# Attention scores of 64-wide heads in split precision: from three matmuls on 64 partitions to two on 128

## The chip, the cores and the metric

The kernel runs on one core of one Trainium2 chip. The metric is the device time of one execution in microseconds (us), the median of several runs. The kernel before takes 2592.72 us (three runs: 2592.72, 2592.72 and 2596.87).

## What is computed

The reference is a stack of four layers over one sequence of 512 tokens of 1024 channels: two layers of a first kind and two of a second, all in fp32. Two parts matter here, one in each kind of layer.

```
# first kind: differential attention, 4 heads, each with two maps m of width 64, v of width 128
scores = einsum('bqhmd,bkhmd->bhmqk', qb, kh)          # causal, block of 128 queries
p = softmax(where(mask, scores, -inf))
w = p[:, :, 0] - lam * p[:, :, 1]
out = einsum('bhqk,bkhd->bqhd', w, vf)

# second kind: sliding-window attention, 8 heads of width 64 over 2 key heads, window 128
sc = (q . k) - slope * distance, masked to the window   # 128 queries see at most 256 keys
p = softmax(concat(sc, sink)); o = p @ v
```

Around them stand large projections (1024 to 8208 columns and to 4256 columns), a state-space scan, a second attention with heads of width 96, and a feed-forward layer.

## The kernel before

All of the program is recorded first, call by call, in an object `Order` (lines 118 to 382). It then issues the calls in the order of a list schedule: each engine takes, among the calls whose operands are there by the schedule's own costs, the one with the highest priority, which is the place in the program with a bonus for weight loads and evictions. Line 379 issues every instruction, so every row of the profile names L379, and groups are told apart by the names of their tiles. The costs of the schedule (line 157, `cost`) do not run on the chip, but they decide in what order each engine's fixed stream stands. For a split-precision matmul of n columns the cost is max(n / 2.4 + 2.5, 109) ns (line 166).

Matmuls that need nearly fp32 accuracy are done in split precision: an fp32 operand is split into a high part (type fp32r, written by ScalarE) and a low part (fp32 minus the high part, by VectorE), and `mm3` (line 501) issues three matmuls, high by high, high by low and low by high, into one PSUM tile. Projections (`tm`, `fm`) contract 128 partitions at a time and write the PSUM tiles `pm`; everything else writes tiles `px`, of which there are four. Weights come from memory as `wr` on SyncE's queue and are split into `wh` and `wl`.

Scores have contraction width 64. In the first kind of layer, `qk_norm` (line 846) transposes q and k on TensorE, two maps of a head on one tile of 128 partitions (map 0 on partitions 0 to 63, map 1 on 64 to 127), and splits each into `qkh` and `qkl`; it also keeps the first 128 tokens in plain fp32 (`qkf`). `da_attn` (line 863) then loops over the four query blocks i, inside over the four heads and the two maps. For i = 0 one plain fp32 matmul on 64 partitions makes the 128x128 scores (TensorE runs it as two passes, so the trace shows two records); for i = 1 to 3 the three matmuls of `mm3` work on 64 partitions with 256, 384 and 512 columns. So a layer has 8 fp32 matmuls (16 records) and 8 x 3 x 3 = 72 split ones: 88 records of 64 partitions. Each score tile goes to VectorE (bias, minimum) and ScalarE (exponential) as `p`, the weighted difference is transposed (`px<-ident,p`), copied to `pt` and multiplied with `vv`.

In the second kind, `swa_norm` (line 1206) and `swa_attn` (line 1228) do the same for the sliding window with tiles `sqth`, `sqtl`, `skth`, `sktl`, `sqf` and `skf`: 8 heads, i = 0 in fp32 with 128 columns, i = 1 to 3 with three matmuls of 256 columns: again 16 + 72 = 88 records a layer. What follows in the program is, in the first kind, the projection for z and the gates, and in the second kind, two gate projections recorded just ahead of it and the attention with heads of width 96 (`mqh`, `mql`, contraction over 96 partitions). The schedule puts matmuls of these projections between the attention's.

GpSimd issues only parameter loads (`pn`, `pa`, `pb`, `pc`, `mw`, `ab`), 25 in all, through its own queue.

Of the kernel before, what the change touches and what calls it, by code (L numbers as in the profile page):

```python
# [19 lines left out]
P = 128  # L20
# [97 lines left out]
class Order:  # L118
    """Records the engine calls of a program, then issues them in the order of a list schedule:
    each engine takes, among the calls whose operands are there, the one that the program has first."""  # L120
# [36 lines left out]
    def cost(self, key, name, out, ins, kw):  # L157
# [4 lines left out]
        if key == "pe":  # L162
            if name == "transpose":
                return 107.0
            if ins[0].dtype == F32R:
                return max(n / 2.4 + 2.5, 109.0)
            return 2 * max(n / 1.2 + 2.5, 109.0)
# [217 lines left out]
class Kern:  # L385
# [173 lines left out]
    def norm(self, x, gain, spill=True):  # L559
        """The rows scaled by the gain only, split in two; their 1/rms by token, as a column and over partitions;  # L560
        and a function that makes the split of the wholly scaled rows."""
# [283 lines left out]

    def qk_norm(self, raw, ms):
        nc = self.nc
        dst = []
# [7 lines left out]
        first = self.slot("qkf")  # L856
        for h in range(4):
            ps = self.transpose_to(raw, h * P)
            nc.scalar.copy(out=first[:, h * P:(h + 1) * P], in_=ps[:, 0:P])
            dst.append(self.split(ps, "qk"))  # L860
        return dst, first

    def da_attn(self, q, qt, kt, v):
        nc = self.nc
        (qt, qf), (kt, kf) = qt, kt
        yc = []
        for i in range(NT):
            n = (i + 1) * P
            o = self.slot("yc")
            for h in range(4):  # L870
# [3 lines left out]
                for m in range(2):  # L874
                    ps = self.pmix()
                    s = slice(m * 64, m * 64 + 64)
                    if i == 0:
                        hs = slice(h * P, (h + 1) * P)
                        nc.tensor.matmul(ps[:, :n], qf[s, hs], kf[s, hs], start=True, stop=True)
                    else:  # L880
                        c = slice(i * P, (i + 1) * P)
                        self.mm3(ps[:, :n], qt[h][0][s, c], qt[h][1][s, c], kt[h][0][s, 0:n], kt[h][1][s, 0:n], True, True)
# [10 lines left out]
                for b in range(i + 1):  # L893
                    nc.tensor.matmul(po[:, 0:P], pt[:, b * P:(b + 1) * P], v[b][:, h * P:(h + 1) * P],
                                     start=(b == 0), stop=(b == i))
                nc.scalar.activation(out=o[:, h * P:(h + 1) * P], in_=po[:, 0:P], func=AF.Copy, scale=rr[:, 0:1])
# [10 lines left out]
            yc.append(o)  # L907
        return yc

    def layer1(self, l, x):  # L910
# [61 lines left out]
        qt = self.qk_norm(qr, msq)  # L972
        kt = self.qk_norm(kr, msk)
        yc = self.da_attn(q, qt, kt, vv)
# [231 lines left out]
    def swa_norm(self, q, sraw, sk, msq, msk):  # L1206
# [11 lines left out]
        qf, kf = self.slot("sqf"), self.slot("skf", [P, P])  # L1218
        ps = self.transpose_to(sk, 0)
        nc.scalar.copy(out=kf, in_=ps[:, 0:P])  # L1220
        kt = self.split(ps, "skt")
        for j in range(4):
            ps = self.transpose_to(sraw, j * P)
            nc.scalar.copy(out=qf[:, j * P:(j + 1) * P], in_=ps[:, 0:P])
            qt.append(self.split(ps, "sqt"))
        return (qt, qf), (kt, kf)

    def swa_attn(self, q, qt, kt, sk, gs, rx):
        nc = self.nc
        (qt, qf), (kt, kf) = qt, kt  # L1230
        y = []
        for i in range(NT):
# [6 lines left out]
            for hp in range(4):  # L1239
                s = hp // 2  # L1240
                sl = slice(s * 64, s * 64 + 64)
                ps = self.pmix()
                for e in range(2):
                    j = (hp * 2 + e) % 4
                    if i == 0:
                        nc.tensor.matmul(ps[:, e * 256:e * 256 + n], qf[sl, j * P:(j + 1) * P], kf[sl, :], start=True, stop=True)
                    else:
                        c = slice(i * P, (i + 1) * P)
# [232 lines left out]
```

## Time and profile before

| | |
|---|---|
| median of the runs | 2592.72 us |
| span of the profiled execution | 2608.1 us (no time of its own is listed beside the span) |
| TensorE matmuls | 2597.5 us, 12708 records |
| weight loads (PEld) | 2191.3 us |
| VectorE | 1587.9 us (61%) |
| ScalarE | 1093.2 us (42%) |
| GpSimd | 13.7 us (1%) |
| DMA | mean 96 GB/s |

The profile is one execution, so its times stand against its own span of 2608.1 us and not against the median. Matmuls are pipelined: the duration that a row shows (0.39 us for 512 columns) reaches into the next one, so TensorE is "busy" all the time, and what a matmul costs is read from the distance between the starts of neighbours in the timeline. In the view by windows, the x after an engine is how many records fall into the stretch, and PEclk is the granted TensorE clock as a share of 2.4 GHz.

### The profile page before, as it was taken

The page shows a single profiled execution, that of the slowest core. Times are in us where ns is not written, and L with a number is a line of the kernel's source. Part 1 is how long each engine was busy: PE and PEld are TensorE (multiplying, and loading weights), DVE is VectorE, ACT ScalarE, POOL GpSimd, SP SyncE. Part 2 cuts the span into 40 slices and gives each one's busy share as a digit, 9 for nine tenths or more (in the row PEclk, how much of TensorE's full clock was granted, in tenths as well). Part 3 has the DMA queues.
Part 4 walks back from the last instruction along what each step waited for, and adds up shares of the span by engine and source line. Part 5 has one row for each costly group of instructions (what it writes and reads, how often), then busy time and mean ns, then how long its engine had stood idle before and what let it go on. Part 6 is the DMA issues. An engine that isn't in the chain of part 4 may idle for free.

```text
span 2608.1 us, 33396 instructions
## 1 busy us (share of the span) xinstructions
PE 2597.5 (100%) x12708; PEld 2191.3 (84%) x12708; DVE 1587.9 (61%) x3165; ACT 1093.2 (42%) x2006; POOL 13.7 (1%) x29
## 2 busy tenths in 40 slices
PE   9999999999999999999999999999999999999999
PEld 7898788888888888987888888888898988988987
DVE  7689843368555356798533585553496655875562
ACT  5443723235443244436332344442345723534632
POOL 0000000000000000000000000000000000000000
PEclk9999999999999999999999999999999999997999
DMA  7333143343333343331333433334432124330132
GB/s 224 79 69 73 40 123 91 95 156 103 97 97 115 130 107 83 80 63 49 89 89 97 132 126 97 96 96 146 135 84 65 28 73 157 100 97 17 33 100 94
DMA packets 154815, 249.79 MB, mean 96 GB/s; under 512 B 10320, under 2 KB 70112, under 8 KB 154400
## 3 DMA queue, kind: packets, MB, share of 16 engines
q1 hardware_dynamic: 152864, 241.03, 33.1%
q0 software_dynamic: 1792, 6.63, 0.8%
q8 instruction: 100, 1.64, 0.3%
q14 instruction: 59, 0.48, 0.1%
HBM read 232.94 MB, written 14.68 MB: 95 GB/s over the span
## 4 chain that ended last, share of the span: by engine, by line
PE 99%; DMA 0%; SPq 0%; ACT 0%; issue 0%; DVE 0%
PE pm L379 76%; PE px L379 23%; DMA wr<-in_w_in_dram 0%; DMA xr<-xd 0%; SPq L379 0%; ACT wh L379 0%; DVE xt L379 0%; ACT pt L379 0%
## 5 line engine op out<-in xcount | busy, mean ns | idle before, releaser
L379 DVE TENSOR_TENSOR wl<-wr,wh 128x1024 fp32r<-128x1024 f32 (+3 forms) x413 | 489.8, 1186 | 836.8 <-ACT wh L379 817.3
L379 ACT CAST wh<-wr 128x1024 fp32r<-128x1024 f32 (+3 forms) x413 | 422.6, 1024 | 1009.7 <-PE pm L379 818.5
L379 PE MATMUL pm<-hh,wl 128*128 128x512 f32 x896 | 349.3, 390 | 0.0
L379 PE MATMUL pm<-hl,wh 128*128 128x512 f32 x896 | 349.1, 390 | 0.0
L379 PE MATMUL pm<-hh,wh 128*128 128x512 f32 x896 | 348.7, 390 | 0.0
L379 PEld LDWEIGHTS pm<-hh,wl 128*128 128x128 f32 x896 | 168.3, 188 | 34.8
L379 PEld LDWEIGHTS pm<-hh,wh 128*128 128x128 f32 x896 | 168.3, 188 | 34.7 <-issue 0.3
L379 PEld LDWEIGHTS pm<-hl,wh 128*128 128x128 f32 x896 | 168.3, 188 | 34.5
L379 PE MATMUL pm<-gh,wh 128*128 128x512 f32 x384 | 153.8, 401 | 0.0
L379 PE MATMUL pm<-gl,wh 128*128 128x512 f32 x384 | 153.6, 400 | 0.0
L379 PE MATMUL pm<-gh,wl 128*128 128x512 f32 x384 | 153.3, 400 | 0.0
L379 PE MATMUL pm<-wh,gh 128*128 128x512 f32 (+2 forms) x384 | 141.4, 371 | 1.4 <-ACT wh L379 1.2
L379 PE MATMUL pm<-wl,hh 128*128 128x384 f32 (+2 forms) x384 | 142.6, 371 | 0.0
L379 PE MATMUL pm<-wl,gh 128*128 128x512 f32 (+2 forms) x384 | 141.5, 369 | 0.0
L379 PE MATMUL pm<-wh,hl 128*128 128x384 f32 (+2 forms) x384 | 141.3, 368 | 0.0
L379 PE MATMUL pm<-wh,hh 128*128 128x384 f32 (+2 forms) x384 | 141.1, 368 | 0.0
L379 PE MATMUL pm<-wh,gl 128*128 128x512 f32 (+2 forms) x384 | 140.9, 368 | 0.0
L379 PE MATMUL pm<-acth,wh 128*128 128x512 f32 x352 | 137.0, 389 | 0.0
L379 PE MATMUL pm<-actl,wh 128*128 128x512 f32 x352 | 137.0, 389 | 0.0
L379 PE MATMUL pm<-acth,wl 128*128 128x512 f32 x352 | 136.7, 389 | 0.0
L379 PE MATMUL px<-hh,wl 128*128 128x512 f32 x320 | 124.6, 389 | 0.0
L379 PE MATMUL px<-hl,wh 128*128 128x512 f32 x320 | 124.6, 389 | 0.0
(440 smaller groups left out, 5156.3 us busy)
## 6 DMA issues: line engine op xcount, KB each, us to landing
wr<-in_w_in_dram SPq DMA_DIRECT2D x151, 512.0 KB, 3.8
wr<-in_ffn_w_up_dram SPq DMA_DIRECT2D x176, 256.0 KB, 3.1
wr<-in_ffn_w_down_dram SPq DMA_DIRECT2D x44, 512.0 KB, 3.5
wr<-in_w_out_dram SPq DMA_DIRECT2D x40, 512.0 KB, 3.6
wr<-in_w_in_dram SPq DMA_DIRECT2D x40, 384.0 KB, 3.6
xr<-xd SPq DMA_DIRECT2D x48, 256.0 KB, 5.0
xd<-xr SPq DMA_DIRECT2D x40, 256.0 KB, 3.7
wr<-in_w_branch_b_dram SPq DMA_DIRECT2D x16, 512.0 KB, 3.5
```

The lines of the kernel that those rows point to most:

```text
L379: ins = f(*args, **kw).ins
```

## The change

Scores are now made by `scores`: two matmuls that contract 128 partitions. The stationary operand is a query tile `qk` (or `sqt`) for one map or head alone, with its high part on one half of the partitions and its low part on the other (`stack_q`). The moving operands are two key tiles, `qkh` and `qkl` (`skth`, `sktl`), each with the same 64 rows on both halves (`stack_k`). The two products give all four terms, high by high, low by high, high by low and low by low. The query's low part is written by VectorE straight to the other half of the partitions; the key's second half is a copy by DMA, 64 rows of 2 KB, issued by GpSimd. The plain fp32 tiles for i = 0 are gone; all four blocks take this way. `da_attn` now loops over heads outside and over query blocks inside, and transposes and stacks a head's q and k at the start of its turn; the norm of the outputs comes after all heads. Lastly the schedule's cost of a split-precision matmul is max(n / 2.4 + 13.4, 109) ns.

```diff
@@ -163,7 +163,7 @@
             if name == "transpose":
                 return 107.0
             if ins[0].dtype == F32R:
-                return max(n / 2.4 + 2.5, 109.0)
+                return max(n / 2.4 + 13.4, 109.0)
             return 2 * max(n / 1.2 + 2.5, 109.0)
         aps = sum(1 for k in ("scale", "bias", "scalar", "scalar1", "scalar2") if isinstance(kw.get(k), bass.AP))
         if key == "act":
...
@@ -843,9 +843,35 @@
             ys.append(yh)
         return ys
 
+    def stack_k(self, ps, rows, name):
+
+        nc = self.nc
+        other = slice(64 - rows.start, 128 - rows.start)
+        h, l = self.slot(name + "h", dt=F32R), self.slot(name + "l", dt=F32R)
+        nc.scalar.copy(out=h[rows, :], in_=ps[rows, :])
+        nc.vector.tensor_sub(out=l[rows, :], in0=ps[rows, :], in1=h[rows, :].bitcast(F32))
+        nc.gpsimd.dma_start(out=h[other, :], in_=h[rows, :])
+        nc.gpsimd.dma_start(out=l[other, :], in_=l[rows, :])
+        return h, l
+
+    def stack_q(self, ps, rows, name):
+
+        nc = self.nc
+        other = slice(64 - rows.start, 128 - rows.start)
+        t = self.slot(name, dt=F32R)
+        nc.scalar.copy(out=t[rows, :], in_=ps[rows, :])
+        nc.vector.tensor_sub(out=t[other, :], in0=ps[rows, :], in1=t[rows, :].bitcast(F32))
+        return t
+
+    HALVES = (slice(0, 64), slice(64, 128))
+
+    def scores(self, ps, q, k):
+        nc = self.nc
+        nc.tensor.matmul(ps, q, k[0], start=True, stop=False)
+        nc.tensor.matmul(ps, q, k[1], start=False, stop=True)
+
     def qk_norm(self, raw, ms):
         nc = self.nc
-        dst = []
         nc.vector.tensor_scalar_add(out=ms, in0=ms, scalar1=EPS)
         r = self.rsqrt(ms, NT * 8)
         for t in range(NT):
...
@@ -853,33 +879,21 @@
             nc.vector.tensor_tensor(out=r3, in0=r3,
                                     in1=r[:, t * 8:(t + 1) * 8].unsqueeze(2).to_broadcast([P, 8, HD]), op=ALU.mult)
             self.rope(r3[:, :, 0:16], 8, 8, self.rope1, t)
-        first = self.slot("qkf")
+    def da_attn(self, q, qr, kr, v):
+        nc = self.nc
+        yc = [self.slot("yc") for _ in range(NT)]
         for h in range(4):
-            ps = self.transpose_to(raw, h * P)
-            nc.scalar.copy(out=first[:, h * P:(h + 1) * P], in_=ps[:, 0:P])
-            dst.append(self.split(ps, "qk"))
-        return dst, first
-
-    def da_attn(self, q, qt, kt, v):
-        nc = self.nc
-        (qt, qf), (kt, kf) = qt, kt
-        yc = []
-        for i in range(NT):
-            n = (i + 1) * P
-            o = self.slot("yc")
-            for h in range(4):
+            hs = slice(h * P, (h + 1) * P)
+            kt, qt = [[f(ps, rows, "qk") for rows in self.HALVES]
+                      for f, ps in ((self.stack_k, self.transpose_to(kr, h * P)), (self.stack_q, self.transpose_to(qr, h * P)))]
+            for i in range(NT):
+                n = (i + 1) * P
                 mn = self.small("mn", 2)
                 ss = self.small("ss", 2)
                 pr = []
                 for m in range(2):
                     ps = self.pmix()
-                    s = slice(m * 64, m * 64 + 64)
-                    if i == 0:
-                        hs = slice(h * P, (h + 1) * P)
-                        nc.tensor.matmul(ps[:, :n], qf[s, hs], kf[s, hs], start=True, stop=True)
-                    else:
-                        c = slice(i * P, (i + 1) * P)
-                        self.mm3(ps[:, :n], qt[h][0][s, c], qt[h][1][s, c], kt[h][0][s, 0:n], kt[h][1][s, 0:n], True, True)
+                    self.scores(ps[:, :n], qt[m][:, i * P:(i + 1) * P], [k[:, 0:n] for k in kt[m]])
                     pr.append(self.softmax_block(ps[:, :n], self.mask[:, T - n:], HD ** -0.5, 3.0e38,
                                                  mn[:, m:m + 1], ss[:, m:m + 1], n))
                 rr = self.small("rr", 2)
...
@@ -891,9 +905,10 @@
                 pt = self.transpose_p(pr[0], i + 1, "s")
                 po = self.pmix()
                 for b in range(i + 1):
-                    nc.tensor.matmul(po[:, 0:P], pt[:, b * P:(b + 1) * P], v[b][:, h * P:(h + 1) * P],
+                    nc.tensor.matmul(po[:, 0:P], pt[:, b * P:(b + 1) * P], v[b][:, hs],
                                      start=(b == 0), stop=(b == i))
-                nc.scalar.activation(out=o[:, h * P:(h + 1) * P], in_=po[:, 0:P], func=AF.Copy, scale=rr[:, 0:1])
+                nc.scalar.activation(out=yc[i][:, hs], in_=po[:, 0:P], func=AF.Copy, scale=rr[:, 0:1])
+        for o in yc:
             ms = self.small("oms", 4)
             sq = self.slot("osq")
             nc.scalar.activation(out=sq, in_=o, func=AF.Square, scale=128 ** -0.5)
...
@@ -969,9 +983,9 @@
         self.tm(w, C_DT + 400, 384, h, ev1)
         self.tm(w, C_DT + 784, 384, h, ev2)
         self.tm(w, C_DT + 1168, 384, h, ev3)
-        qt = self.qk_norm(qr, msq)
-        kt = self.qk_norm(kr, msk)
-        yc = self.da_attn(q, qt, kt, vv)
+        self.qk_norm(qr, msq)
+        self.qk_norm(kr, msk)
+        yc = self.da_attn(q, qr, kr, vv)
         msz = self.small("msz", 2 * NT)
 
         def ev_z(hf):
...
@@ -1215,19 +1229,15 @@
             nc.vector.tensor_tensor(out=s3, in0=s3, in1=rq[:, t * 8:(t + 1) * 8].rearrange("p (s j) -> p s j", s=2).unsqueeze(3).to_broadcast([P, 2, 4, HD]), op=ALU.mult)
             k3 = sk[t][:, 0:128].rearrange("p (s d) -> p s d", d=HD)
             nc.vector.tensor_tensor(out=k3, in0=k3, in1=rk[:, t * 2:(t + 1) * 2].unsqueeze(2).to_broadcast([P, 2, HD]), op=ALU.mult)
-        qf, kf = self.slot("sqf"), self.slot("skf", [P, P])
         ps = self.transpose_to(sk, 0)
-        nc.scalar.copy(out=kf, in_=ps[:, 0:P])
-        kt = self.split(ps, "skt")
+        kt = [self.stack_k(ps, rows, "skt") for rows in self.HALVES]
         for j in range(4):
             ps = self.transpose_to(sraw, j * P)
-            nc.scalar.copy(out=qf[:, j * P:(j + 1) * P], in_=ps[:, 0:P])
-            qt.append(self.split(ps, "sqt"))
-        return (qt, qf), (kt, kf)
+            qt.append([self.stack_q(ps, rows, "sqt") for rows in self.HALVES])
+        return qt, kt
 
     def swa_attn(self, q, qt, kt, sk, gs, rx):
         nc = self.nc
-        (qt, qf), (kt, kf) = qt, kt
         y = []
         for i in range(NT):
             ss = self.small("sss", 8)
...
@@ -1238,16 +1248,11 @@
             k0 = max(i - 1, 0) * P
             for hp in range(4):
                 s = hp // 2
-                sl = slice(s * 64, s * 64 + 64)
                 ps = self.pmix()
                 for e in range(2):
                     j = (hp * 2 + e) % 4
-                    if i == 0:
-                        nc.tensor.matmul(ps[:, e * 256:e * 256 + n], qf[sl, j * P:(j + 1) * P], kf[sl, :], start=True, stop=True)
-                    else:
-                        c = slice(i * P, (i + 1) * P)
-                        self.mm3(ps[:, e * 256:e * 256 + n], qt[j][0][sl, c], qt[j][1][sl, c],
-                                 kt[0][sl, k0:k0 + n], kt[1][sl, k0:k0 + n], True, True)
+                    self.scores(ps[:, e * 256:e * 256 + n], qt[j][s][:, i * P:(i + 1) * P],
+                                [k[:, k0:k0 + n] for k in kt[s]])
                 pp = []
                 for e in range(2):
                     h = hp * 2 + e
```

The schedule makes a new order from this. Three places show it. In the first layer's attention, TensorE's stream of before holds the block i = 1 of two heads so (`px_647` and `px_649` are the two maps of a head, `qkh_583` the keys, `pm` a projection):

```order
L379 MATMUL pm_815<-wh_823,hh_197 128x512
L379 MATMUL px_647<-qkh_583,qkh_559 128x256
L379 MATMUL px_647<-qkl_584,qkh_559 128x256
L379 MATMUL px_647<-qkh_583,qkl_560 128x256
L379 MATMUL px_649<-qkh_583,qkh_559 128x256
L379 MATMUL px_649<-qkl_584,qkh_559 128x256
L379 MATMUL px_649<-qkh_583,qkl_560 128x256
L379 MATMUL px_658<-qkh_586,qkh_562 128x256
L379 MATMUL px_658<-qkl_587,qkh_562 128x256
L379 MATMUL px_658<-qkh_586,qkl_563 128x256
L379 MATMUL pm_815<-wl_824,hh_197 128x512
```

Of the change, the first head's first scores stand so; `DMASW` is the semaphore of a copy that GpSimd issued:

```order
L379 MATMUL pm_804<-wh_812,hh_203 128x512
L379 MATMUL px_582<-qkh_574,qk_578 128x128 [waits DMASW2_49,DVE_49]
L379 MATMUL px_593<-qkh_574,qk_578 128x256 [waits DVE_49]
L379 MATMUL pm_804<-wl_813,hh_203 128x512
L379 MATMUL pm_804<-wh_812,hl_204 128x512
L379 MATMUL pm_804<-wh_812,hh_206 128x512
L379 MATMUL px_582<-qkl_575,qk_578 128x128 [waits DMASW3_49]
L379 MATMUL px_593<-qkl_575,qk_578 128x256
L379 MATMUL pm_804<-wl_813,hh_206 128x512
```

Each score tile takes two matmuls where it took three, and a head's blocks stand close together. Between the last key transpose of this head and the first row that waits for a copy stand 20 matmuls of 512 columns and 6 transposes; for the fourth head it is 21 and 17. GpSimd's stream, which held only a parameter load here, now has these copies:

```order
L379 DMA pn_1563<-in_pn_dram 128x8
L379 DMA qkh_574<-qkh_574 64x512
L379 DMA qkl_575<-qkl_575 64x512
L379 DMA qkh_576<-qkh_576 64x512
L379 DMA qkl_577<-qkl_577 64x512
L379 DMA qkh_626<-qkh_626 64x512
```

In all it is 16 copies in each layer of the first kind and 4 in each of the second. In the sliding window, TensorE's stream of before has a transpose of another head between two score tiles of 64 partitions:

```order
L379 MATMUL px_3332<-skth_3246,sqth_3249 128x256
L379 MATMUL px_3332<-sktl_3247,sqth_3249 128x256
L379 MATMUL px_3332<-skth_3246,sqtl_3250 128x256
L379 MATMUL px_3306<-ident_75,p_3305 128x128
L379 MATMUL px_3332<-skth_3246,sqth_3252 128x256
L379 MATMUL px_3332<-sktl_3247,sqth_3252 128x256
L379 MATMUL px_3332<-skth_3246,sqtl_3253 128x256
L379 MATMUL pm_3640<-gh_3007,wh_3644 128x512
```

and of the change, at the same block of queries:

```order
L379 MATMUL pm_3654<-gh_3017,wh_3656 128x512
L379 MATMUL px_3330<-ident_75,p_3328 128x128
L379 MATMUL px_3350<-skth_3256,sqt_3267 128x256
L379 MATMUL px_3350<-sktl_3257,sqt_3267 128x256
L379 MATMUL px_3350<-skth_3256,sqt_3270 128x256
L379 MATMUL px_3330<-ident_75,p_3329 128x128
L379 MATMUL px_3350<-sktl_3257,sqt_3270 128x256
L379 MATMUL pm_3654<-gl_3018,wh_3656 128x512
```

The two heads of a tile still follow each other, with two matmuls each. Between the last key transpose and the first scores of this layer stand 126 matmuls of 512 columns.

## Rows read from the trace of the kernel before

**Rows 1.** The page: engines (busy us, share of the span, instructions), the chain by engine.
```profile
PE 2597.5 (100%) x12708; PEld 2191.3 (84%) x12708; DVE 1587.9 (61%) x3165; ACT 1093.2 (42%) x2006; POOL 13.7 (1%) x29
...
PE 99%; DMA 0%; SPq 0%; ACT 0%; issue 0%; DVE 0%
```
**Rows 2.** The chain in order of time (start us, us, what): one projection stretch.
```profile
313.61 91.61 PE pm L379 x404
```
**Rows 3.** TensorE's timeline (start us, us, engine, line, instruction): one fp32 score.
```profile
260.70 0.40 PE L379 MATMUL pm<-wh,hh 128*128 128x512 f32 x1
261.03 0.49 PE L379 MATMUL px<-qkf,qkf 64*128 64x128 f32 x2
261.44 0.50 PE L379 MATMUL pm<-wl,hh 128*128 128x512 f32 x1
261.79 0.40 PE L379 MATMUL pm<-wh,hl 128*128 128x512 f32 x1
```
**Rows 4.** TensorE's timeline: split scores of two maps, 256 columns.
```profile
269.64 0.40 PE L379 MATMUL px<-qkh,qkh 64*128 64x256 f32 x2
269.87 0.28 PE L379 MATMUL px<-qkl,qkh 64*128 64x256 f32 x2
...
270.33 0.27 PE L379 MATMUL px<-qkh,qkl 64*128 64x256 f32 x1
270.54 0.50 PE L379 MATMUL pm<-wl,hh 128*128 128x512 f32 x1
```
**Rows 5.** TensorE's timeline: fp32 and 96-partition matmuls of the other attention.
```profile
2067.96 1.00 PE L379 MATMUL px<-v,pt 128*128 128x64 f32 x8
2068.80 0.49 PE L379 MATMUL px<-ident,k 128*96 128x128 f32 x3
...
2069.36 1.47 PE L379 MATMUL px<-ident,k 128*96 128x128 f32 x12
2070.59 0.49 PE L379 MATMUL pm<-gh,wl 128*128 128x512 f32 x1
...
2074.26 0.28 PE L379 MATMUL px<-mqh,mqh 96*128 96x256 f32 x1
2074.38 0.28 PE L379 MATMUL px<-mql,mqh 96*128 96x256 f32 x1
```
**Rows 6.** By windows (stretch, us, PE busy, clock, DMA), TensorE, tile pm.
```profile
260.00:310.00 50.00, 23.16 (x71) 1.00 0.11 32
1990.00:2032.00 42.00, 14.02 (x47) 1.00 0.09 26
```
**Rows 7.** By windows, TensorE, tile ident (the transposes).
```profile
260.00:310.00 50.00, 6.76 (x38) 1.00 0.11 32
1990.00:2032.00 42.00, 9.55 (x53) 1.00 0.09 26
```
**Rows 8.** By windows, TensorE, tile vv.
```profile
260.00:310.00 50.00, 10.23 (x64) 1.00 0.11 32
```
**Rows 9.** By windows, TensorE, tile spt.
```profile
1990.00:2032.00 42.00, 11.95 (x88) 1.00 0.09 26
```
**Rows 10.** By windows, TensorE, all tiles: a stretch at half clock, the next.
```profile
2355.90:2393.30 37.40, 37.40 (x135) 0.50 0.05 15
2393.40:2430.00 36.60, 36.60 (x278) 1.00 0.06 16
```
**Rows 11.** By tile (duration ns min/median/max): ScalarE's and VectorE's parts of a split.
```profile
L379 ACT CAST qkh<-px x16: 592/620/662, 245.9 to 1189.4; 128x512 fp32r<-128x512 f32 x16
...
L379 DVE TENSOR_TENSOR qkl<-px,qkh x16: 681/685/692, 246.5 to 1195.9; 128x512 fp32r<-128x512 f32 x16
```
**Rows 12.** By windows, VectorE alone: the first attention.
```profile
255.00:340.00 85.00, 66.52 (x232) 1.00 0.27 69
```
**Rows 13.** By tile, GpSimd's loads mw: from issue to landing.
```profile
DMA to landing us min/median/max: 2.5/3.5/5.7
```
**Rows 14.** By tile, GpSimd's loads ab: from issue to landing.
```profile
DMA to landing us min/median/max: 4.6/6.0/7.5
```

## What the change is expected to do, recorded before its time was known

> **What bounds the kernel now.** The page comes first: TensorE is busy for 2597.5 of 2608.1 us, VectorE for 61% and ScalarE for 42% of the span, and the chain of work that ended last lies on TensorE to 99% [rows 1]. So time goes away only where TensorE's stream gets shorter, and comes in only where that stream waits. But a busy TensorE is not yet a well used one, since a record's duration reaches into its neighbour. What a matmul takes must be read from the distance of starts. The chain in order of time has stretches that are nothing but projections: 404 matmuls in 91.61 us, 0.227 us for one of 512 columns [rows 2]. I use that as the price of a matmul on the whole array. The timeline of the second attention gives the small ones: 8 fp32 records of 64 columns from 2067.96 to 2068.80, 0.105 us each; 12 transposes from 2069.36 to 2070.59, 0.10 us each, of which I take 0.11 with what the neighbours add; and a split matmul of 256 columns that contracts 96 partitions, 0.12 us from 2074.26 to 2074.38 [rows 5]. For 384 columns I take 0.173 us, halfway between 0.12 and 0.227: an estimate.
>
> Then the timeline of the scores. The fp32 score at 261.03 starts 0.33 us after a projection matmul that needs 0.227; the next projection starts 0.41 us later, and the one behind it after 0.35 us more [rows 3]. From 260.70 to 261.79 lies 1.09 us, of which two projections account for 0.45: one 128x128 score costs 0.64 us, though two records at 0.11 make 0.22. The same shows at 256 columns: from 270.33 to 270.54 there are 0.21 us where the price is 0.12 [rows 4]. Each time the stream goes from the whole array to 64 rows or back, about 0.1 us is lost, again at the first projection behind. On the other side, two maps on different halves of the rows start together: the records at 269.64, 269.87 and on stand as x2 [rows 4].
>
> What all of this costs follows from a balance. From 260 to 310 us TensorE issues all 88 score records of the first layer's attention (16 in fp32 and 72 split), 71 projections, 38 transposes and 64 records with vv [rows 6 to 8]. At the prices above the others take 71 x 0.227 + 102 x 0.11 = 16.1 + 11.2 = 27.3 us. The 88 scores have the rest of the 50 us: 22.7 us. From 1990 to 2032 us it issues the 88 scores of a sliding window, with 47 projections, 53 transposes and 88 records with spt [rows 6, 7, 9]: 10.7 + 5.8 + 9.2 = 25.7 us, and 42 less that leaves 16.3 us. Two layers of each kind: 2 x (22.7 + 16.3) = 78.0 us of the span go to 64-row scores.
>
> **The change part by part.** Removed are these 352 records with all entries and exits of the 64-row state. Added are 256 matmuls on 128 rows. In a layer of the first kind a map of a head takes 2 x (0.11 + 0.12 + 0.173 + 0.227) = 1.26 us, eight of them 10.1 us. In the second kind a head takes 2 x (0.11 + 3 x 0.12) = 0.94 us, eight 7.5 us. That is 2 x (10.1 + 7.5) = 35.2 us, and the difference is 42.8 us. Of the added forms one has no row: split matmuls of 128 columns, 64 in number. Nearest from below is the transpose of 128 columns at 0.10, from above an fp32 product of that size, two records at 0.11. I take 0.11; the upper end adds 64 x 0.11 = 7.0 us, the lower takes off 0.6.
>
> A rule of the Trainium skill speaks against this sum. "TensorE: Matmul & The Clock Gate", part 3 on packing small matmuls, says that matmuls on different row groups of the array run at the same time, so that 64-row scores would be half price and stacking them on 128 rows would give that up. The trace shows the concurrency [rows 4], yet the balance finds the scores dearer and not cheaper than their columns; by that rule alone it would come out slower, and the last rival has the time.
>
> The schedule's new cost and the loop over heads move the whole order. Outside the attention this has nothing to win: the projection stretch above runs without a gap already. It can lose: the schedule used to believe a projection matmul 11 ns shorter than it now does, so every operand had some 11 ns more time per matmul in between than planned. With about 20 matmuls between a hand-off and its use, as between the first head's transposes and scores, that is 0.2 us of cover less per hand-off. VectorE and ScalarE get more work: stacking a head takes four high copies and four low parts of 64 rows for two of each on 128 rows, at 0.62 and 0.685 us if rows do not matter [rows 11]. That is 8 x 0.685 = 5.5 us more VectorE in a first-kind layer, where it is busy for 66.5 of 85 us [rows 12] and the stretch loses 12.6 us: 72 of 72.4 us. The projections that follow hide it: attention can run on beside them, since its output is used only at the third gate. If that cover is gone, the excess beyond the stretch, a microsecond or two, becomes TensorE's wait.
>
> New is a wait of TensorE's stream on GpSimd's copies. Behind the waiting score stand all the projections of the stretch, so a late copy stops the engine. For the first head, 20 matmuls and 6 transposes cover it: 20 x 0.227 + 6 x 0.11 = 5.2 us; for the fourth 21 x 0.227 + 17 x 0.11 = 6.6 us. Needed are a ScalarE copy of 0.62 us and the transfer. GpSimd's loads land 2.5 to 5.7 us after issue, 3.5 in the median [rows 13], and 4.6 to 7.5 where four stand in a row [rows 14]; none of them is a copy inside the chip's buffer, and 128 KB is less than either. So 3.1 to 8.1 us are needed: no stall at one end, 2.9 + 1.5 = 4.4 us in each of two layers at the other, 8.8 us in all. In the sliding window 126 matmuls are cover enough (28.6 us). By the median it is 4.1 us and fits; I take 1 us for the copies and 3 us for tighter hand-offs, as TensorE's idle time before is nil [rows 1]; the hand-offs' upper end is 8 us, 0.2 us at 40 of them.
>
> A second rule bears on the copies. "SBUF — State Buffer", in the section on its two sides, warns that GpSimd cannot write the descriptors of its transfers while VectorE runs certain copies on a port that both share. GpSimd's rows of 2.5 to 7.5 us were taken beside such a VectorE and are not told apart by it; should the rule bite, the copies tend to the upper end.
>
> Where the sum starts: the profiled execution had a stretch from 2355.9 to 2393.3 us at a granted clock of 0.50, which is 1.2 GHz [rows 10]. TensorE got through 135 records there and through 278 in the next 36.6 us at 2.4 GHz. It came within a sliding window, with TensorE on 64-row scores, transposes and few projections. At most half of 37.4 us is lost by it, 18.7 us; the profiled span is 15.4 us over the median of the runs. I read this as a fall that the median execution does not have. The change then makes 2592.7 - 42.8 + 4 = 2553.9 us; with a fall like the profile's 2608.1 - 38.8 = 2569.3 us.
>
> **Rivals.** First, the clock falls in the timed executions. For it: it did so once in four attentions of the profile. Against it: the rows at which it did, 64-row scores, are gone, and the stretches have as many projections. The time is 2569.3 us as above, 2560 to 2578 with the copies.
>
> Second, late copies and tight hand-offs together at their upper ends, with the 128-column matmuls at the fp32 price: 8.8 + 8 + 7 = 23.8 us in place of 4, 2592.7 - 42.8 + 23.8 = 2573.7 us. For it speaks that the scheduled cover has under a microsecond above the median copy, against it that each of the three would have to be at its end.
>
> Third, slower: the 0.1 us steps around 64-row records are not the array's doing but waits for operands from VectorE and ScalarE, and stay, while the concurrency goes. At streaming price the 88 scores are 16 x 0.11 + 24 x (0.12 + 0.173 + 0.227) = 14.2 us in the first kind and 16 x 0.11 + 72 x 0.12 = 10.4 us in the second; side by side half of it, 12.3 us for a layer of each, and two of each kind 24.6 us. Then 78.0 - 24.6 = 53.4 us are waits, and after the change 53.4 + 35.2 = 88.6 us: 10.6 us more, 2603 us. It decides from the point where waits are over 42.8 us of the 78. Against it: at 261.44 to 261.79 it is a projection whose operands have long been there that starts late [rows 3]. That the change does not do what it says is excluded: its stream has 256 score matmuls, each on 128 rows.
>
> **How the numbers follow.** The forecast, 2554 us, holds in 0.62 of cases with its own range of 2545 to 2562. The clock's fall has 0.20, the late copies 0.11, the slower case 0.04, and 0.03 is left for more than these numbers foresee above 2580. The range of 2544 to 2577 takes in the first two and most of the third, and leaves out about 0.15. A change of less than 0.2%, 5 us, could not be told from none. Faster by more than that is 0.62 + 0.20 + 0.11 and half of what is unforeseen, 0.94; within it 0.02; slower 0.04.
>
> **What would show it.** In the profile after, no record of 64 rows; score records of 128 rows at distances of 0.12, 0.17 and 0.23 us, and no 0.1 us before and behind them; 128 columns at 0.11. The balance of the first attention would leave about 10 us for 64 scores, that of the sliding window 7.5 us. TensorE's wait for a DMA before the first head's and the fourth head's scores under 1 us each. The prediction is wrong if the clock falls once in most runs, if idle time of TensorE in the first attention is over 3 us a layer, or if score records on 128 rows stay at a distance that their columns do not explain.

## The result and the profile after

The changed kernel takes 2572.26 us (median of four, 2570.47 to 2573.04), the kernel before, beside it, 2594.8 us (2592.72 to 2609.56); the ratio is 0.9899, 95% interval [0.9865, 0.9933]. The forecast was 2554 us with a range of 2544 to 2577: faster as said, inside the range, but 20.5 us under the 2592.72 it started from and not 39. The kernel before has executions near 2592 us and some near 2609 us, whose mean granted clock of 0.993 agrees with a half-clock stretch as in [rows 10]; the ratios' base is a mean of both, so differences in us below are taken from 2592.7.

The profiled execution of the changed kernel took 2572.86 us with a span of 2571.1. Its page, engines and chain by engine, against [rows 1]:

```profile
PE 2550.3 (99%) x12612; PEld 2168.2 (84%) x12612; DVE 1599.3 (62%) x3191; ACT 1101.3 (43%) x2006; POOL 34.4 (1%) x69
...
PE 92%; DVE 5%; DMA 1%; ACT 1%; issue 0%; SPq 0%; POOLq 0%; DVEq 0%
```

The 96 records less are the 352 that went and the 256 that came. What is new is the chain: 8% of it lies off TensorE, where it was 1%.

TensorE's timeline in the first attention after, against [rows 3, 4] (start us, duration us, instruction):

```profile
285.31 0.22 PE L379 MATMUL px<-qkh,qk 128*128 128x128 f32 x1
285.37 0.27 PE L379 MATMUL px<-qkl,qk 128*128 128x128 f32 x1
285.48 0.45 PE L379 MATMUL pm<-wh,hh 128*128 128x512 f32 x1
285.77 0.39 PE L379 MATMUL pm<-wl,hh 128*128 128x512 f32 x1
286.00 0.83 PE L379 MATMUL px<-vv,pt 128*128 128x128 f32 x6
286.58 0.36 PE L379 MATMUL px<-qkh,qk 128*128 128x256 f32 x1
286.78 0.28 PE L379 MATMUL px<-qkl,qk 128*128 128x256 f32 x1
286.90 0.28 PE L379 MATMUL px<-qkh,qk 128*128 128x256 f32 x1
287.02 0.28 PE L379 MATMUL px<-qkl,qk 128*128 128x256 f32 x1
287.14 0.39 PE L379 MATMUL pm<-wh,hl 128*128 128x512 f32 x1
```

From 285.31 to 285.77 lies 0.46 us, of which the projection takes 0.227: a score of 128 columns now costs 0.23 us where the fp32 one took 0.64. At 256 columns the records follow each other after 0.12 us, from the second on. The first one starts 0.58 us after six records with `vv`, but there the sum comes out too: from 286.00 to 287.14 lies 1.14 us, and 6 x 0.11 + 4 x 0.12 = 1.14. Single distances still differ by up to 0.1 us; what the visit of a score costs beyond its columns, as in [rows 3, 4], is gone.

Those scores are as cheap as forecast. What is not as forecast is TensorE's waits (engine, tile, releaser: us in total, times, longest):

```profile
PE px L379 <- DMA xin<-in_x_dram: 4.7, 3, 4.1
PE px L379 <- ACT yc L379: 1.9, 3, 1.0
PE px L379 <- DVE sraw L379: 1.9, 2, 1.0
PE pm L379 <- DVE zs L379: 1.8, 2, 1.0
PE px L379 <- DMA cst<-in_cst_dram: 1.0, 1, 1.0
PE px L379 <- ACT pt L379: 1.0, 2, 0.8
...
PE px L379 <- DVE k L379: 0.7, 2, 0.3
PE px L379 <- DMA qkl<-qkl: 0.6, 1, 0.6
```

The kernel before shows `xin`, at the start of the program, in that size, 1.2 us for `wh`, and nothing else over 0.2 us. `cst` belongs to the start as well; `yc`, `zs` and `pt` belong to the first kind's attention, `sraw` to the second kind, `k` to the other attention. The copies of the keys cost 0.6 us. The largest group, from TensorE's timeline of the first attention, with the idle time and its releaser in brackets:

```profile
265.16 0.39 PE L379 MATMUL pm<-wl,hh 128*128 128x512 f32 x1
265.39 0.40 PE L379 MATMUL pm<-wh,hl 128*128 128x512 f32 x1
265.62 0.61 PE L379 MATMUL px<-vv,pt 128*128 128x128 f32 x4
267.19 0.55 PE L379 MATMUL px<-ident,p 128*128 128x128 f32 x3 [0.96 <-ACT yc L379]
267.49 0.48 PE L379 MATMUL px<-qkh,qk 128*128 128x512 f32 x1
267.81 0.40 PE L379 MATMUL px<-qkl,qk 128*128 128x512 f32 x1
268.36 0.94 PE L379 MATMUL px<-vv,pt 128*128 128x128 f32 x6 [0.16 <-ACT pt L379]
269.75 0.33 PE L379 MATMUL px<-qkh,qk 128*128 128x128 f32 x1 [0.46 <-ACT yc L379]
269.92 0.28 PE L379 MATMUL px<-qkl,qk 128*128 128x128 f32 x1
270.96 0.50 PE L379 MATMUL pm<-wh,hh 128*128 128x512 f32 x1 [0.77 <-DVE zs L379]
```

For 5.3 us no projection is in the stream, and without them TensorE follows the chain of one softmax after another. ScalarE's timeline of that moment tells what the projections were missing:

```profile
269.33 0.37 ACT L379 ACTIVATE yc<-px,rr 128x128 f32<-128x128 f32 x1 [1.03 <-PE px L379]
269.60 1.56 ACT L379 ACTIVATE zs<-pm 128x512 f32<-128x512 f32 x3
```

Three finished projections are evicted in one go, `pm` to `zs`, though ScalarE had been idle for 1.03 us just before. They could not be evicted earlier, and the experiments ask why.

### The profile page after: what moved, and what is told of

It is laid out like the page before. It is cut to its first block, busy times and chain, and to the rows that moved or that the text cites. A ratio compares the mean times of both kernels' runs of the same rounds, so it can differ in the third digit from the quotient of the medians.

```text
span 2571.1 us, 33407 instructions
## 1 busy us (share of the span) xinstructions
PE 2550.3 (99%) x12612; PEld 2168.2 (84%) x12612; DVE 1599.3 (62%) x3191; ACT 1101.3 (43%) x2006; POOL 34.4 (1%) x69
## 4 chain that ended last, share of the span: by engine, by line
PE 92%; DVE 5%; DMA 1%; ACT 1%; issue 0%; SPq 0%; POOLq 0%; DVEq 0%
PE pm L379 72%; PE px L379 21%; DVE wl L379 1%; DVE q L379 1%; DMA pb<-in_pb_dram 0%; DVE k L379 0%; DMA cst<-in_cst_dram 0%; DVE sraw L379 0%; DVE m2q L379 0%; DVE qk L379 0%; ACT wh L379 0%; DMA wr<-in_w_in_dram 0%; DVE rb L379 0%; DVE m2k L379 0%; DVE ra L379 0%
## 5 line engine op out<-in xcount | busy, mean ns | idle before, releaser
L379 PE MATMUL px<-hh,wh 128*128 128x512 f32 x320 | 124.5, 389 | 0.0
```

The lines of the kernel that those rows point to most:

```text
L379: ins = f(*args, **kw).ins
```

## The experiments

All kernels are the changed one with the edit shown, except where said. Each was run in five rounds beside the kernel before; ratios are against that.

**e1: the old price.** First the obvious rivals. Theory 1: the schedule's new price of a matmul (line 166) lets operands come late; theory 2: one head at a time does it; theory 3: the copies through GpSimd's queue.

```diff
-                return max(n / 2.4 + 13.4, 109.0)
+                return max(n / 2.4 + 2.5, 109.0)
```

> The change with one edit undone: the schedule's cost of a split matmul is again n / 2.4 + 2.5 ns. Theory 1 (the new cost takes the cover of hand-offs away, and that is where about 20 us of the 43 went): the time falls to about 2553 us, and TensorE's waits in the state-space scan, the attention and the second kind of layer go to near nothing. Theory 2 (one head at a time puts dependent steps too close) and theory 3 (the key copies are late): 2572 us, within 3 us, with the same waits.

2554.58 us (2554.29 to 2555.14), ratio 0.9808 [0.9779, 0.9837]. The one number costs 17.7 us; without it the change gives 38.1 us, where 38.8 were forecast. TensorE's waits in this kernel, complete:

```profile
PE px L379 <- DMA xin<-in_x_dram: 4.3, 2, 4.1
PE px L379 <- DMA qkh<-qkh: 0.7, 1, 0.7
PE pm L379 <- ACT wh L379: 0.6, 1, 0.6
PE px L379 <- DVE sqt L379: 0.3, 2, 0.2
PE px L379 <- ACT yc L379: 0.2, 1, 0.2
```

**e2: the new price alone**, in the kernel before (the same line, the other way).

> The kernel before with only the schedule's cost changed to n / 2.4 + 13.4 ns; scores as before. Theory 1: slower than before by 10 to 25 us, 2603 to 2618 us, with waits of TensorE in the state-space scan. Theories 2 and 3: 2593 us, within 4 us, as before.

2598.95 us (2596.35 to 2641.68), ratio 1.0001 [0.9971, 1.003]. By the lowest runs, 2596.35 against 2592.24, it costs 4.1 us here: less than theory 1 said, and at the upper edge of what theories 2 and 3 said. Of its waits:

```profile
PE px L379 <- DVE sraw L379: 1.9, 2, 1.0
...
PE px L379 <- DMA cst<-in_cst_dram: 0.9, 1, 0.9
PE px L379 <- DVE k L379: 0.7, 2, 0.3
```

These are the waits of the changed kernel outside the attention of the first kind, nearly to the tenth. So some 4 of the 17.7 us look like late operands that the price brings to either version, and most of the other 13.6 come only with the changed attention.

**e3: token blocks outside**, all heads stacked first, new price.

```diff
-        for h in range(4):
-            kt, qt = [...]
-            for i in range(NT):
+        kqs = [[...] for h in range(4)]
+        for i in range(NT):
+            for h in range(4):
+                kt, qt = kqs[h]
```

> The change with the first kind's attention looped as before: all four heads are transposed and stacked first, then query blocks outside and heads inside. Theory 2: 2564 us, as the waits of 4 to 5 us in each first-kind attention go. Theory 1: 2572 us, within 3 us. Theory 3: not below 2572 us, since sixteen copies are then queued ahead of the first scores.

2600.86 us (2598.11 to 2602.62), ratio 0.9995 [0.9973, 1.0016]: 28.6 us slower than the changed kernel. Theory 2 falls, and the other way round: the order by heads saves time. Theory 1's 2572 us is missed as well.

**e4: no copies.** The key's second half is written by ScalarE and VectorE.

```diff
-        nc.gpsimd.dma_start(out=h[other, :], in_=h[rows, :])
-        nc.gpsimd.dma_start(out=l[other, :], in_=l[rows, :])
+        nc.scalar.copy(out=h[other, :], in_=ps[rows, :])
+        nc.vector.tensor_sub(out=l[other, :], in0=ps[rows, :], in1=h[rows, :].bitcast(F32))
```

> The change with the key's second half made by ScalarE and VectorE straight from the transposed keys instead of by GpSimd's copies: 20 more copies of 64 rows on ScalarE and 20 more subtractions on VectorE in a pair of layers. Theory 3: 2568 us or less, as the wait for the copies (0.8 us seen once) and the delay that it starts go. Theories 1 and 2: 2572 us to 2578 us, since VectorE, full in this stretch, has 5.5 us more to do in a first-kind layer.

2577.09 us (2575.57 to 2578.09), ratio 0.9895 [0.9868, 0.9921], 4.8 us slower: theory 3 falls, and at this price the copies are the cheaper way.

**e5: three matmuls again**, old price.

```diff
         nc.tensor.matmul(ps, q, k[0], start=True, stop=False)
+        nc.tensor.matmul(ps, q, k[1], start=False, stop=False)
         nc.tensor.matmul(ps, q, k[1], start=False, stop=True)
```

> The changed kernel with the schedule's price of a matmul back at n/2.4 + 2.5 ns, and with a third matmul per score: the query stack against the low part of the keys is issued twice, so that the terms of the low key part enter the scores twice. It tells apart what made the scores cheaper, three matmuls becoming two or the 64-row state going away. If the state was the cost, the third matmul on 128 rows costs only its columns: 128 more matmuls, 2 x (4.7 + 3.4) = 16.3 us at 0.07, 0.12, 0.173 and 0.227 us for 128 to 512 columns, so 2554.6 + 16.3 = 2571 us, 2566 to 2577. If the count was the whole gain, the kernel returns to that of before, 2590 to 2596 us.

2570.76 us (2570.36 to 2571.55), ratio 0.9882 [0.9853, 0.9912]. Against e1 the third matmul costs 16.2 us, its columns' 16.3 (17.6 if 128 columns are put at 0.11 us and not at 0.07). With three matmuls on 128 rows the kernel still gains 22 us of the 38; the rest comes from the matmul saved. The 22 us are not the 64-row state alone: the plain fp32 scores of the first block went with it, and the order by heads came with it, which e11 below puts at up to 3.5 us. So the state is worth about half of the gain.

**e6: token blocks outside, old price** (e3's edit with e1's).

> The changed kernel with the price back at n/2.4 + 2.5 ns and the loops of before, token blocks outside and heads inside, so that all four heads are stacked ahead of the first score. Theory 1, that the price without slack is what lets late operands stop TensorE: with the old price the order of the loops matters little, 2554 to 2562 us. Theory 2, that stacking all heads first makes a peak of work on VectorE and ScalarE which stops TensorE whatever the price: the 28 us between the two loop orders stay, 2578 to 2586 us.

2619.61 us (2616.43 to 2622.84), ratio 1.007 [1.0044, 1.0097]. Theory 1 is wrong in this form: with the old price the order of the loops is worth 65 us, not nothing. Theory 2's range, 2578 to 2586 us, is passed by 34 us too. By windows (stretch, length, busy us and records of PE, PEclk, DMA share, GB/s), TensorE's `pm` tiles:

```profile
258.90:305.00 46.10, 0.23 (x1) 0.54 0.25 47
```

In the same stretch e1 has 124 projections and the kernel before has 65. Here none starts for 46 us (the one record counted began at 258.73), at a granted clock of 0.50 for most of it; in the second layer's attention none starts from 1213.1 to 1258 us.

**The heap.** Which tile do projections wait for? All work tiles of 512 columns come from one heap of 68 slots (`NSLOT`, line 26), and the schedule does not place a call whose output finds no slot that earlier calls of the program can spare. A projection beside the attention is evicted to a slot (`zs`). The kernel before holds 18 slots for its heads' queries and keys; four stacked heads hold 24, one stacked head 6. `schedule` can be run by itself, since it is arithmetic of the program. In the plan of the changed kernel three evictions `zs<-pm` are ready at 249.4, 251.0 and 252.8 us. The schedule turns them away for want of a slot until 258.9, and starts them at 259.2, 259.7 and 260.1, one behind the other as in ScalarE's timeline above. The plan also says where TensorE has nothing to do in the attentions of the first kind, from the first score to the last product with `vv`; these are planned times by its own prices, not the chip's:

| kernel | planned idle in the two attentions, us | measured, us | over e1 |
|---|---|---|---|
| before; e11; e2 | 0 | 2592.7; 2590.9; 2596.4 (lowest) | |
| e1; e5 | 0 | 2554.6; 2570.8 | 0; its third matmul |
| e8 | 0 | 2558.2 | 3.6 |
| e12 | 0 + 7.2 | 2564.4 | 9.8 |
| e7 | 5.3 + 4.9 | 2563.5 | 8.9 |
| after | 4.1 + 3.5 | 2572.3 | 17.7 |
| e4 | 3.1 + 4.5 | 2577.1 | 22.5 |
| e10 | 13.7 + 6.2 | 2588.3 | 33.7 |
| e3 | 16.4 + 16.2 | 2600.9 | 46.3 |
| e6 | 28.1 + 28.1 | 2619.6 | 65.0 |
| e9 | 37.0 + 37.2 | 2650.6 | 96.0 |

The plan tells which kernels lose and roughly in what order, not how much: e7 is planned with more idle time than after and loses half of what it loses. With 76 slots in place of 68 the plans of after, e3, e4, e6, e7, e10 and e12 have none of this idle time. That was not run; e9 takes slots away instead.

A part of the last column is the clock, which in these kernels fell in or right behind stretches without projections, and in some at the start. Before the last 10 us of the program the granted clock stood at 0.50 for 116 us in e9's profiled execution, 82 in e6's, 27 in e3's and e10's, 10 in e12's and that of after, 7 in e4's, 3 in e7's, and never in e1's and e8's; at most half of each is lost by it.

**e9: ten slots held** during the attention, one head at a time, old price.

```diff
         yc = [self.slot("yc") for _ in range(NT)]
+        held = [self.slot("held") for _ in range(10)]
+        for o in held:
+            nc.vector.tensor_copy(out=o[:, 0:1], in_=kr[3][:, 511:512])
...
+        for o in held:
+            nc.vector.tensor_add(out=self.small("hd", 1), in0=o[:, 0:1], in1=yc[3][:, 511:512])
         for o in yc:
```

> The changed kernel with the old price and one head at a time, but with ten of the 68 slots of the heap taken from the last step before the attention to its end (ten copies and ten additions of one column on VectorE, some 2 us a layer of the first kind, are added; the result does not change). Slot theory: with token blocks outside, the 24 slots of four stacked heads fill the heap, no gate projection beside the attention gets its output slot, and TensorE is left with the softmax's chain alone; then it must happen here too although heads go one at a time, 2585 to 2625 us. Peak theory: what hurt there was the work of stacking all heads at once; then this kernel stays at 2554 to 2562 us.

2650.61 us (2649.51 to 2652.99), ratio 1.0177 [1.015, 1.0204]: 96 us over e1, beyond the slot theory's own range. The added copies and additions take VectorE 0.144 and 0.151 us each, 3 us a layer. TensorE's `pm` by windows, then all its tiles in that stretch:

```profile
260.80:305.20 44.40, 0.00 (x0) 0.50 0.13 29
...
260.80:305.20 44.40, 26.78 (x82) 0.50 0.13 29
```

No projection at all, with heads one at a time and at half clock throughout: taking slots away is enough, and the peak theory falls.

**e7: a lower price.** `n / 2.4 - 8.4`.

> The changed kernel with a price of n/2.4 - 8.4 ns, 10.9 ns under the old one, so that the schedule plans every matmul shorter still and operands have more time than planned. If slack is what matters, it is as good as with the old price, 2552 to 2557 us. If the old price was the right one and a deviation on either side costs, about as much as the new price, 2562 to 2575 us.

2563.48 us (2561.27 to 2565.92), ratio 0.9855 [0.9823, 0.9887]: 8.9 us over e1. More slack in the price is not better.

**e8: the others' prices up 5%**, new price of a matmul kept (all of VectorE's and ScalarE's returns in `cost` times 1.05).

> The changed kernel with the new price of a matmul kept and the schedule's prices of VectorE and ScalarE raised by 5%. Theory 1a, that the new price is near what a matmul takes but stands beside prices of the other engines that are too low, so that their operands come later than planned: the loss goes, 2553 to 2561 us. Theory 1b, that the matmul's new price is itself what makes a bad order: it stays, 2569 to 2576 us.

2558.19 us (2557.01 to 2559.9), ratio 0.9834 [0.9805, 0.9863], as theory 1a said. Its premise is not borne out, though. In e1's trace VectorE starts its next instruction 600 ns after one of 512 elements whose price is 600, and ScalarE some 515 to 535 ns after one priced 519; only their records, 685 and 630 ns, are longer. The prices were about right on all engines, the matmul's new one too (226.7 ns for 512 columns, 0.227 us in [rows 2]). What e8 restores is the ratio between them, and its plan has no idle time in the attentions.

**e10: a margin per hand-off**, new price.

```diff
-    HOPS = {("pe", "act"): 197.0, ("pe", "dve"): 196.0, ...
-            ("act", "pe"): 270.0, ("dve", "pe"): 285.0}
+    HOPS = {("pe", "act"): 297.0, ("pe", "dve"): 296.0, ...
+            ("act", "pe"): 370.0, ("dve", "pe"): 385.0}
```

> The changed kernel with its new price of a matmul, and 100 ns more in the schedule for each hand-off between TensorE and VectorE or ScalarE, either way. Margin theory: the exact price leaves operands no margin, and a margin given per hand-off is as good as one given in the price: 2553 to 2562 us. Ratio theory: what helps is that TensorE is priced 4 to 5% too fast against the other engines, which adds up along a queue, and a fixed time per hand-off doesn't replace it: 2566 to 2576 us.

2588.33 us (2584.38 to 2589.72), ratio 0.9929 [0.9906, 0.9953]. Both theories missed, on the slow side. TensorE's timeline:

```profile
264.52 0.45 PE L379 MATMUL pm<-wh,hl 128*128 128x512 f32 x1
268.12 0.33 PE L379 MATMUL px<-ident,p 128*128 128x128 f32 x1 [3.16 <-DVE p L379]
268.81 0.80 PE L379 MATMUL px<-vv,pt 128*128 128x128 f32 x2 [0.36 <-ACT pt L379]
...
274.31 0.69 PE L379 MATMUL px<-ident,p 128*128 128x128 f32 x2 [2.14 <-DVE p L379]
...
281.07 0.80 PE L379 MATMUL pm<-wh,hh 128*128 128x512 f32 x1 [1.26 <-DVE zs L379]
```

It is the picture of the changed kernel, longer: 16.5 us from one projection to the next, ended by `zs`, in the attention for which the plan has 13.7 us of idle time. I read it so that a planned margin makes tiles live longer and the heap fill sooner; that was not tried by itself.

**e11: heads outside in the kernel before**, 64-row scores and old price kept; only the loops and the place of the split move.

> The kernel before with its 64-row scores, three products each and its old price, and only the loops of the first kind's attention turned round: one head at a time, its split made just before its scores. Slot theory: the kernel before holds 18 slots for its heads and still got 71 projections beside its attention, so the order of loops alone is worth little: 2586 to 2597 us. If one head at a time is a gain of its own, which the changed kernel would then owe it: 2565 to 2580 us.

2590.85 us (2589.01 to 2608.28), ratio 0.9955 [0.9933, 0.9977]. Lowest against lowest it is 3.5 us under the kernel before (2592.52). The order by heads is worth little where slots suffice.

**e12: half the price step.** `n / 2.4 + 8.0`.

> The changed kernel with a price of n/2.4 + 8 ns, halfway between the old one's 2.5 and the new one's 13.4. If the loss grows with the price, the time lies between the two: 2558 to 2568 us. If each price merely makes another order, good or bad by chance, anything from 2553 to 2576 us can come, and a value outside 2555 to 2572 us would say so.

2564.4 us (2563.59 to 2566.25), ratio 0.9846 [0.982, 0.9872]: between the two, as a loss growing with the price would have it. Its profile says otherwise. TensorE's waits in its first attention (237 to 345 us), all of them, and then in its second (1155 to 1245):

```profile
PE px L379 <- ACT pt L379: 0.2, 1, 0.2
...
PE px L379 <- ACT pt L379: 2.4, 3, 1.4
PE px L379 <- ACT yc L379: 1.4, 3, 0.5
PE pm L379 <- DVE zs L379: 0.5, 1, 0.5
PE px L379 <- DVE qk L379: 0.2, 1, 0.2
```

The first is clean and the second has the chain of the softmax ended by `zs`, as in the plan (0 and 7.2 us). So the price did not dose the loss here; it decided whether a given attention ran out of slots.

## Why the forecast was right in kind and short by half

**The scores: right, with some luck in the sum.** 42.8 us were taken off, 4 given back; e1, which has all of the change but the price, gives 38.1 for the 38.8. But 3 of the 4 us stood for hand-offs that the new price makes tighter, and e1 does not have that price. Its waits for stacked operands, copies and `yc` come to 1.2 us, so the scores themselves gave about 39.3 us, some 3.5 under the 42.8, and the unused term covered the difference. The chief rival explanation, that the 0.1 us steps were waits of operands, had 2603 us and falls with e1 and e5. The rule on packing that spoke against the sum (the Trainium skill, "TensorE: Matmul & The Clock Gate", part 3) describes a concurrency that [rows 4] show, but by it alone the kernel had to get slower; e1's ratio of 0.9808 decides against it here.

**The balances.** By windows from 260 to 310 us, TensorE's tiles `pm`, `ident` and `vv` after, against [rows 6 to 8]:

```profile
260.00:310.00 50.00, 31.99 (x114) 1.00 0.29 77
...
260.00:310.00 50.00, 6.78 (x39) 1.00 0.29 77
...
260.00:310.00 50.00, 9.21 (x62) 1.00 0.29 77
```

114 x 0.227 + 101 x 0.11 = 37.0 us; 13.0 us are left for 56 of the 64 score records, for which the forecast's prices make 9.1. The other 3.9 us hold the 2.35 us of waits from 267 to 271 us shown above. In the sliding window, with no such waits, 97 projections and 208 small records (88 with `ident`, 112 with `spt`, 8 with `mqf`) leave 7.1 of 52 us for 60 score records, against 7.1 by the forecast's prices (from 1985 to 2037 us).

**The price of 128 columns: right.** Starts lie 0.06 and 0.11 us apart at 285.31, but the projection behind takes 0.29 us in place of 0.227. With it, two records cost 0.23 us, where 0.22 was taken.

**VectorE's extra work: right.** The prediction had 72 us of work for a stretch of 72.4, with the projections as cover. From the first score to the last product with `vv` the first layer's attention did not get shorter but longer, 64.6 us after 52.3, because 157 projections stand in it where 72 stood. So the work spread; by windows, VectorE alone:

```profile
255.00:340.00 85.00, 70.96 (x235) 1.00 0.39 92
```

**The copies: right, and the bound was too dear.** 1 us was taken. By tile, `qkh` of the changed kernel:

```profile
DMA to landing us min/median/max: 2.2/2.9/4.9
```

They land sooner than the loads of [rows 13, 14], and TensorE's one wait for them is 0.6 us. They ran beside a VectorE busy for 71 of 85 us, and the rule on the shared port (the Trainium skill, "SBUF — State Buffer", the section on its two sides) was not seen to bite. It was not tested either: VectorE's operations within 3 us of each issue, in all 40 cases, are subtractions and steps of the softmax, and none is a plain copy (`COPY`), such as the rule names.

**The step that failed** is the 3 us for "tighter hand-offs". It was sized as a fixed loss per hand-off, with 8 us as its upper end, and the projections were taken as cover that is always there: "attention can run on beside them". The price cost 17.7 us. Taken by stretches, as time beyond what the matmuls need at the rows' prices, the changed kernel loses against e1 about 3.0 us in the first layer's attention (238 to 345 us), 7.5 in the second's (1155 to 1250), 1.4 at the start, and 5.8 in the scans, the second kind of layer and bits. What lies outside the attentions, 7.2 us, holds the hand-offs that e2 shows: over twice the 3 us taken, and inside the upper end of 8. The 10.5 us inside hold 1.3 us of waits for stacked operands and a copy. Most of the others come of a mechanism that was not in the prediction at all: the cover itself needs slots, and where the heap of 68 is full, projections stop and the softmax's chain sets the pace. The forecast's own warning sign, over 3 us of idle time a layer, came in the second layer (3.3 us of waits from 1160 to 1250 us) and nearly in the first (2.7 from 238 to 335). Why 10.9 ns a matmul tip this order over and 5.5 ns only one of two attentions was not worked out beyond the plan.

**The clock.** It fell twice in the changed kernel: at the start, behind the 1.0 us wait for `cst` (0.50 from 31.8 to 35.2 us, a part of the 1.4), and in the second attention, after the waits:

```profile
1194.00:1196.00 2.00, 1.24 (x8) 0.91 (x8) 2.00 (x6) 1.63 (x5) 0.00 (x0) 0.94 0.17 24
1196.00:1202.00 6.00, 5.24 (x12) 4.13 (x13) 6.00 (x15) 5.28 (x17) 1.02 (x2) 0.50 0.47 125
```

Columns are busy us of PE, weight loads, DVE, ACT and POOL, then the clock. TensorE was busy for 1.24 of 2 us before. These 6.8 us at half clock cost at most 3.4 us, part of the 7.5; a fall like that of [rows 10], the first rival, did not come, and yet a loss of the size that it priced, 15.4 us, came from elsewhere. (That price set a span against a time; time against time, the two kinds of runs of the kernel before lie 17 us apart.) The range held in part by that accident.

## What to carry to other kernels

Read what a stretch's cover needs before counting on it: here projections hid the attention only while the shared heap had slots for their outputs. Count the tiles that a change holds, and look in the plan of the order for the bound engine's idle time, which `schedule` could have told beforehand. And when several edits come together, time the one that "only" moves the order by itself: the score edit without the new price is the best version found, 2554.6 us.

## What the runs showed of the hardware

- Scores on 64 rows, placed between matmuls on the whole array, cost TensorE more than their columns explain: e5 issues three split matmuls for a score on 128 rows, as the kernel before does on 64 from the second block on, and is 22 us faster (up to 3.5 of them by the order of the loops, e11), while its third matmul on 128 rows costs 16.2 us, no more than its columns explain.
- A copy of 64 rows of 2 KB inside the chip's buffer, issued by GpSimd, landed in 2.2 to 4.9 us; GpSimd was busy 0.52 us for each issue.
- In e6 the granted clock stood at 0.50 for 47.8 us from 262.0 us, while TensorE was busy 35.5 of them between waits, and was full again at 309.8, after projections had come back at 308.2. In [rows 10] it stood at 0.50 under a TensorE that showed no waits.
